# More buffers, a warm-up tile set by VectorE, a last tile ended in quarters, and new engine orders in a hybrid trunk layer

## The chip, the cores and the metric

The kernel runs on one core of one Trainium2 chip. The time is that of one execution on the device in microseconds (us), the median of several runs. Engines are called as in the profile: PE (TensorE), DVE (VectorE), ACT (ScalarE), POOL (GpSimd) and SP (SyncE, which issues the DMAs here).

## The reference

One layer over 1024 positions of width 1024, in float32. One projection gives the columns of three groups, each group's output is gated, and one output projection and a LayerNorm over the residual sum end the layer.

```python
proj = jnp.einsum("bsd,de->bse", x, w_in[l])
q, k, v, g_a, x_b, g_b, c_cols, g_c = jnp.split(proj, split_idx, axis=-1)
y_a = _swa_sinks(q, k, v, attn_sinks[l])      # 8 heads on 2 kv heads of 64, window 128, a sink per head
y_b = _rg_lru(x_b, ...)                       # causal convolution, gates, linear recurrence over time
y_c, v_own = _rwkv7(c_cols, ...)              # delta rule with a matrix state, 4 heads of 64
y = jnp.concatenate([y_a * silu(g_a), y_b * silu(g_b), y_c * silu(g_c)], axis=-1)
out = jnp.einsum("bse,ed->bsd", y, w_out[l])
x = _layer_norm(ALPHA * x + out, ln_g[l], ln_b[l])
```

## The kernel before

The 1024 positions are worked in two halves `h` of 512 columns, and the 1024 input rows in eight slices. Float32 products are made of rounded high parts and remainders: a product is three matmuls (high by high, high by low, low by high), so every activation (`xh`, `xl`) and every weight is split by a cast on ACT or DVE (`wcah`, `woh`) and a subtraction on DVE (`wcal`, `wol`).

*Start.* Four warm-up matmuls of 256 columns run on the tile `blocks`, which POOL sets; POOL makes of the same tile the block matrix `hsum`, used later for head sums. Behind them the seven tiles of the C group's projection (`c0`) are made straight from the loads, slice by slice. *Dense groups.* The remaining projections (tiles named `q0`, `ga0`, `xb1` and so on, in the order of the list `LISTED`) follow. In the first half their weights come into a raw tile (4 buffers), are split into a weight tile `w_...` (4 buffers) and written to DRAM; in the second half SP loads the split weights back from there (`w_ga<-kept_ga`, 512 KB each) as soon as a weight tile is free. *Side streams.* Among the dense matmuls lie the small ones. `scores_stream` makes scores of 128 queries (`sp`), masks them and sums them up in `mn` on DVE and takes the exponential on ACT into `s`; `turn_stream` transposes `s` on PE (`tp`) and puts the result, masked, into `PT`; `pv_stream` multiplies by the values (`pv`). The C group has per half eight chunks in series: a first `ch` from the state and the chunk's `X`, a copy to `u0`, a second `ch` with the transposed inverse `Tt`, a copy to `UV`, a third `ch` with `BKt`, and the new state `S`; `yp` is the chunk's output. The B group has its recurrence as a scan on DVE. The products with the output weights (`o`) and the normalisation of eight tiles of 128 positions (`finish`) end the program. The gates of a projection (`evac_gate`) and `PT` have fixed numbers of buffers, which set how far a stream may run ahead.

*Order.* Every helper records its instructions (`Listed`), so all rows carry line 231, or 253 in the changed kernel. The program is first written by `merge`, which draws from the streams by the string `MERGED`; then the table `ISSUED` gives, for every engine, the sequence of the recorded instructions, and each engine runs strictly by it. A matmul that must wait holds up all behind it on PE.

`finish` before:

```python
P.tensor_tensor(mv[:, 3:4], mv[:, 2:3], mhalf, op=ALU.pow)
for js in halves:
    V.scalar_tensor_tensor(xr[:, js], xr[:, js], mv[:, 0:1], lng[:, js], op0=ALU.subtract, op1=ALU.mult)
for js in halves:
    V.scalar_tensor_tensor(xr[:, js], xr[:, js], mv[:, 3:4], lnb[:, js], op0=ALU.mult, op1=ALU.add)
    SQ.dma_start(out[t0:t0 + 128, js], xr[:, js])
```

Of the kernel before, what the change touches and what calls it, by code (L numbers as in the profile page):

```python
# [10 lines left out]
F32 = mybir.dt.float32  # L11
# [10 lines left out]
T = 512  # L22
# [12 lines left out]
PVN = 2  # L35
C0 = (1, 4, 3, 0, 6, 2, 5)
# [10 lines left out]
NS = 3  # L47
NGATE = 2
# [1288 lines left out]
```

## Time and profile before

| | |
|---|---|
| median of 3 runs | 482.28 us (481.49 to 482.39) |
| profiled execution | 482.19 us |
| its span | 480.4 us |
| PE busy | 466.0 us, 97%, 3088 records |
| DVE busy | 364.7 us, 76% |
| ACT busy | 242.4 us, 50% |
| POOL busy | 36.4 us, 8% |
| bytes moved | 71.45 MB, 149 GB/s over the span |

Busy time is the sum of an engine's instructions in the span. Matmuls are pipelined: a record's duration is longer than the distance to the next one's start, so for PE the distances between starts are what counts. A line of the timeline may hold several equal instructions (x2, x8); its duration then covers them all. What stands in brackets is the idle time before and the instruction or transfer that ended it.

### The profile page before, as it was taken

The numbers are of one execution on the slowest core, as the hardware profiler recorded it, in microseconds if no ns is written. First come the engines' busy times: TensorE is split into PE (matmuls) and PEld (weight loads), VectorE is DVE, ScalarE is ACT, GpSimd is POOL, SyncE is SP. The second block draws the span as 40 slices with busy tenths as digits, with TensorE's granted clock in tenths as the row PEclk, the third lists the DMA queues.
The fourth block names the chain that finished last, engine by engine and source line by source line (L and its number), as shares of the span: only waits on it lengthen the run. The fifth ranks groups of instructions, "written<-read, shape, count | busy, mean of one in ns | idle before, by whom it ended". The sixth has DMA issues, their size and how long they took to land.

```text
span 480.4 us, 8435 instructions
## 1 busy us (share of the span) xinstructions
PE 466.0 (97%) x3088; PEld 360.8 (75%) x3088; DVE 364.7 (76%) x880; ACT 242.4 (50%) x544; POOL 36.4 (8%) x57
## 2 busy tenths in 40 slices
PE   8999999999999999999999998999999999999993
PEld 6777777777777776678778786787678778888893
DVE  5946798999998689737979669994868548636886
ACT  3427589434566798537694255329666546021000
POOL 0100000000000000000000000000002500054101
PEclk9999999999999999999999999999999999999997
DMA  8950537657766524233343484459420080120652
GB/s 275 386 200 0 196 136 264 199 130 262 268 238 130 189 91 132 89 114 128 99 167 88 141 233 153 132 119 220 134 67 24 16 283 32 64 69 0 219 176 87
DMA packets 50585, 71.45 MB, mean 149 GB/s; under 512 B 26344, under 2 KB 27624, under 8 KB 50544
## 3 DMA queue, kind: packets, MB, share of 16 engines
q1 hardware_dynamic: 50544, 70.91, 46.3%
q8 instruction: 24, 0.39, 0.4%
q14 instruction: 17, 0.14, 0.1%
HBM read 48.34 MB, written 22.56 MB: 148 GB/s over the span
## 4 chain that ended last, share of the span: by engine, by line
PE 74%; DVE 9%; ACT 7%; DMA 6%; issue 2%; SPq 1%; POOLq 0%; DVEq 0%; ACTq 0%
PE o L231 19%; PE pj_q L231 8%; PE pj_ga L231 6%; PE c L231 6%; PE pj_xb L231 3%; PE pj_gb L231 3%; PE pj_gc L231 3%; PE sp L231 3%; PE pv L231 3%; PE pj_v L231 2%; PE pj_r L231 2%; PE ch L231 2%; PE pj_av L231 2%; PE tp L231 2%; PE pj_k L231 2%
## 5 line engine op out<-in xcount | busy, mean ns | idle before, releaser
L231 PE MATMUL pj_ga<-xh,w_ga 128*128 128x512 f32 x128 | 44.0, 404 | 0.9 <-DMA w_ga<-kept_ga 0.9
L231 PE MATMUL pj_q<-xh,w_q 128*128 128x512 f32 x128 | 44.1, 403 | 0.5 <-DMA w_q<-kept_q 0.2
L231 ACT ACTIVATE s<-sp,mn 128x129 f32<-128x129 f32 x64 | 23.0, 366 | 22.0 <-DVE mn L231 21.7
L231 PE MATMUL o<-woh,yl 128*128 128x512 f32 (+1 forms) x90 | 32.5, 370 | 0.0
L231 PE MATMUL o<-woh,yh 128*128 128x512 f32 (+1 forms) x90 | 32.5, 375 | 0.0
L231 PE MATMUL o<-wol,yh 128*128 128x512 f32 (+1 forms) x90 | 32.3, 368 | 0.0
L231 PE MATMUL o<-wo,yh 128*128 128x512 f32 (+1 forms) x108 | 32.0, 374 | 0.0
L231 PEld LDWEIGHTS pj_ga<-xh,w_ga 128*128 128x128 f32 x128 | 23.6, 188 | 7.6 <-DVE it L231 1.2
L231 POOL TENSOR_TENSOR yl<-y,yh 128x512 fp32r<-128x512 f32 x16 | 20.3, 1291 | 118.0 <-PE pj_gc L231 105.5
L231 PEld LDWEIGHTS pj_q<-xh,w_q 128*128 128x128 f32 x128 | 23.8, 188 | 7.0 <-DMA w_q<-kept_q 0.7
L231 DVE SCALAR_TENSOR_TENSOR xres<-xres,o 128x512 f32<-128x512 f32 (+1 forms) x18 | 11.1, 624 | 20.3 <-PE o L231 16.2
L231 PE MATMUL pj_ga<-xl,w_ga 128*128 128x512 f32 x64 | 25.9, 405 | 0.0
L231 PE MATMUL pj_q<-xl,w_q 128*128 128x512 f32 x64 | 25.7, 401 | 0.0
L231 ACT ACTIVATE s<-s,mn 128x128 f32<-128x128 f32 x64 | 22.3, 398 | 4.3 <-DVE mn L231 4.1
L231 DVE SCALAR_TENSOR_TENSOR xres<-xres,mv,ln 128x512 f32<-128x512 f32 x32 | 22.6, 741 | 1.0 <-POOL mv L231 0.9
L231 PE MATMUL pj_gc<-xh,w_gc 128*128 128x512 f32 x64 | 23.1, 414 | 0.2 <-DVE q L231 0.2
L231 ACT CAST yh<-y 128x512 fp32r<-128x512 f32 x16 | 9.7, 618 | 26.6 <-PE o L231 22.1
L231 PEld LDWEIGHTS o<-wo,yh 128*128 128x128 f32 x108 | 19.4, 188 | 4.2 <-DVE wo L231 0.3
L231 PE MATMUL pj_gb<-xh,w_gb 128*128 128x512 f32 x64 | 21.8, 404 | 0.0
L231 PE MATMUL pj_xb<-xh,w_xb 128*128 128x512 f32 x64 | 21.8, 399 | 0.0
L231 DVE TENSOR_TENSOR PT<-tp,con 128x512 f32<-128x512 f32 x28 | 19.1, 684 | 3.4 <-PE tp L231 3.2
L231 PE MATMUL o<-wo,yl 128*128 128x512 f32 (+1 forms) x54 | 19.8, 369 | 0.0
(310 smaller groups left out, 1247.1 us busy)
## 6 DMA issues: line engine op xcount, KB each, us to landing
xr<-in_xT SPq DMA_DIRECT2D x16, 256.0 KB, 4.5
kept_ga<-w_ga SPq DMA_DIRECT2D x8, 512.0 KB, 3.2
kept_q<-w_q SPq DMA_DIRECT2D x8, 512.0 KB, 3.5
wor<-in_w_o SPq DMA_DIRECT2D x16, 256.0 KB, 2.8
w_q<-kept_q SPq DMA_DIRECT2D x8, 512.0 KB, 3.9
w_ga<-kept_ga SPq DMA_DIRECT2D x8, 512.0 KB, 4.4
xres<-in_x SPq DMA_DIRECT2D x8, 512.0 KB, 3.6
out<-xres SPq DMA_DIRECT2D x16, 256.0 KB, 2.2
```

What stands on the lines that cost most here:

```text
L231: self.ins.append(getattr(self.engine, op)(*args, **kw).ins)
```

## The change

The rings get more buffers: `PT` 4 to 6 (`PTB`, with the value tile `vt` and the output streams' use of the ring), scores `s` 3 to 5 (`NS`) and `mn` 4 to 6, gates 2 to 3, raw weights 4 to 5. The warm-up matmuls use a tile of their own, `warm`, set by DVE, and `blocks` shrinks to the 128 columns of `hsum`. In `finish` the last tile's second pass and its stores go by quarters of 256 columns. All lists of `ISSUED` but none of `MERGED` or `LISTED` are new; each engine gets the same work apart from the edits above (two more passes and stores, one more memset).

```diff
+PTB = 6
-NS = 3
-NGATE = 2
+NS = 5
+NGATE = 3
 ISSUED = {
 "tensor": (
-    "0-3 7 10-11 8 4-6 19-20 22-23 13 24-25 21 26 39-43 9 14-15 33-35 27 44-45 53-54 28-29 47 12 30-32 50-51 48 "
...
 "sync": (
-    "0 2 11 1 3-6 10 28 7-9 13 12 14-16 29-31 17-22 33 32 23-26 44-45 34 46 48 27 47 50 52 51 53-54 49 35-36 "
...
+    "0 2 1 10 3-4 28 5-9 13 29-30 14-15 12 16-17 31 18-23 11 34 24 32 44 25 46 26 48 27 33 47 50 45 52 35 54 49 "
...
-        return s(pers, "raw", shape, 4, F32, name)
+        return s(pers, "raw", shape, 5, F32, name)
...
-    blocks = s(first, "blocks", [128, 256], 1)
+    warm = s(first, "warm", [128, 256], 1)
+    V.memset(warm, 0.0)
+    blocks = s(first, "blocks", [128, 128], 1)
     P.memset(blocks, 0.0)
     for o in (0, 64):
         P.memset(blocks[o:o + 64, o:o + 64], 1.0)
 
     for _ in range(WARM):
-        TE.matmul(start_ps[6][:, 0:256], blocks[:, 0:128], blocks, start=True, stop=True)
-    P.tensor_copy(hsum, blocks[:, 0:128])
+        TE.matmul(start_ps[6][:, 0:256], warm[:, 0:128], warm, start=True, stop=True)
+    P.tensor_copy(hsum, blocks)
...
-        g = wt("gate", bufs=2, name=f"G_{name}_{h}")
+        g = wt("gate", bufs=3, name=f"G_{name}_{h}")
...
-    NS = 3
...
-        VT[0] = wt("PT", (128, T), 4, name=f"vt_{h}")
+        VT[0] = wt("PT", (128, T), PTB, name=f"vt_{h}")
...
-                    mn = wt("mn", (128, 4), 4, name=f"mn_{h}_{g}_{n}")
+                    mn = wt("mn", (128, 4), NS + 1, name=f"mn_{h}_{g}_{n}")
...
-            yield lambda: len(AQ) > i and len(BQ) - got("pv") + got("vt") < 4
+            yield lambda: len(AQ) > i and len(BQ) - got("pv") + got("vt") < PTB
...
-            PT = wt("PT", (128, 2, 2, 128), 4, name=f"PT_{h}_{g}_{n}")
+            PT = wt("PT", (128, 2, 2, 128), PTB, name=f"PT_{h}_{g}_{n}")
...
-        bufs = {"xs": XSB, "lt": 4, "q": 2, "PT": 4, "AR": 2, "rt": 6}
+        bufs = {"xs": XSB, "lt": 4, "q": 2, "PT": PTB, "AR": 2, "rt": 6}
...
-        for js in halves:
+        for js in quarters if (h, i) == (1, 3) else halves:
             V.scalar_tensor_tensor(xr[:, js], xr[:, js], mv[:, 3:4], lnb[:, js], op0=ALU.mult, op1=ALU.add)
             SQ.dma_start(out[t0:t0 + 128, js], xr[:, js])
```

Three places of the orders follow. Names end in a running number; `h` is the first number of a name behind its tag.

PE at the start of the program, before (`c0_1` to `c0_6` are tiles of the C projection, `wcah` the split weights of slice 0):

```order
L231 MATMUL c0_6_69<-blocks_76 128x256 x4
L231 MATMUL c0_2_70<-xh_0_0_95,wcah_0_89 128x512
L231 MATMUL c0_3_67<-xh_0_0_95,wcah_0_89 128x512
L231 MATMUL c0_3_67<-xl_0_0_96,wcah_0_89 128x512
L231 MATMUL c0_2_70<-xl_0_0_96,wcah_0_89 128x512
L231 MATMUL c0_1_65<-xh_0_0_95,wcah_0_89 128x512
L231 MATMUL c0_1_65<-xl_0_0_96,wcah_0_89 128x512
```

PE at the start, in the changed kernel:

```order
L253 MATMUL c0_6_69<-warm_76 128x256
L253 MATMUL c0_1_65<-xh_0_0_97,wcah_0_91 128x512
L253 MATMUL c0_6_69<-warm_76 128x256
L253 MATMUL c0_4_66<-xh_0_0_97,wcah_0_91 128x512
L253 MATMUL c0_6_69<-warm_76 128x256
L253 MATMUL c0_2_70<-xh_0_0_97,wcah_0_91 128x512
L253 MATMUL c0_3_67<-xh_0_0_97,wcah_0_91 128x512
L253 MATMUL c0_4_66<-xl_0_0_98,wcah_0_91 128x512
L253 MATMUL c0_2_70<-xl_0_0_98,wcah_0_91 128x512
L253 MATMUL c0_6_69<-warm_76 128x256
L253 MATMUL c0_6_69<-xh_0_0_97,wcbh_0_93 128x512
```

The four warm-up matmuls now read `warm` and stand one by one among the first matmuls of the C projection, instead of all ahead of them.

DVE at the start, in the changed kernel (`xh_0_0` and `xl_0_0` are the split of the first loaded slice):

```order
L253 MEMSET dv_410 128x1
L253 MEMSET carry_452 128x8
L253 MEMSET ec_425 128x2
L253 CAST xh_0_0_97<-xr_0_0_95 128x512
L253 MEMSET warm_76 128x256
L253 TENSOR_TENSOR xl_0_0_98<-xr_0_0_95,xh_0_0_97 128x512
```

The memset of `warm` is the fifth instruction of DVE, behind the first cast.

DVE around the copy of the transposed inverse `Tt` of the second half, before (`ti` and `tr` belong to the B group's recurrence, and the row `tr_1_1` with `hlast` is its scan):

```order
L231 SCALAR_TENSOR_TENSOR q3_1_3965<-pj_q3_1_3912,q3_1_3965 64x512 x2
L231 COPY u0_1_0_3716<-ch_1_0_3710 128x128
L231 SCALAR_TENSOR_TENSOR ti_1_1_3501<-ti_1_1_3501,xc_1_1_3470 128x512
L231 SCALAR_TENSOR_TENSOR tr_1_1_3500<-a_1_1_3506,hlast_452,ti_1_1_3501 128x512
L231 COPY Tt_1_3622<-tp_1_3634 32x16x32
L231 SCALAR_TENSOR_TENSOR y_1_5_3515<-tr_1_1_3500,G_gb1_1_3426 128x512
L231 SCALAR_TENSOR_TENSOR y_1_0_3577<-pv_1_0_3323,G_ga0_1_3558 128x512
```

DVE around the same copy in the changed kernel:

```order
L253 COPY_PREDICATED sp_1_2_0_3827<-con_63,sp_1_2_0_3827 128x2x128
L253 COPY sp_1_2_0_3827<-par_64 128x2
L253 TENSOR_REDUCE mn_1_2_0_3826<-sp_1_2_0_3827 128x2
L253 RECIPROCAL mn_1_2_0_3826<-mn_1_2_0_3826 128x2
L253 COPY u0_1_0_3718<-ch_1_0_3712 128x128
L253 SCALAR_TENSOR_TENSOR y_1_1_3757<-pv_1_1_3581,G_ga1_1_3744 128x512
L253 COPY Tt_1_3624<-tp_1_3636 32x16x32
L253 COPY_PREDICATED sp_1_2_1_3842<-con_63,sp_1_2_1_3842 128x2x128
L253 TENSOR_TENSOR PT_1_2_0_3873<-tp_1_2_0_3870,con_63 128x512
```

The scan, directly ahead of the copy before, stands 16 rows ahead of it now; between them are attention's masks and sums and the copy of `u0`.

PE at chunk 5 of the second half, from the chunk's first `ch` to its second, before:

```order
L231 MATMUL ch_1_5_4311<-UV_1_2989,X_1_2865 64x64 x4
L231 MATMUL yp_1_5_4312<-AR_1_0_2596,S_1_4_4283 64x64 x2
L231 MATMUL yp_1_5_4312<-AR_1_1_2853,S_1_4_4283 64x64 x2
L231 MATMUL tp_1_3_1_4047<-con_63,s_1_3_1_3987 128x128 x2
L231 MATMUL o_0_3_0_4492<-woh_4_0_3012,yh_0_4_4494 128x512
L231 MATMUL o_0_3_0_4492<-wol_4_0_3013,yh_0_4_4494 128x512
L231 MATMUL o_0_3_0_4492<-woh_4_0_3012,yl_0_4_4495 128x512
L231 MATMUL pv_1_3_4190<-PT_1_3_0_4020,vtok_457 64x128 x4
L231 MATMUL pv_1_3_4190<-PT_1_3_1_4050,vtok_457 64x128 x4
L231 MATMUL ch_1_5_4311<-u0_1_5_4317,Tt_1_3622 64x64 x4
```

PE at the same chunk in the changed kernel:

```order
L253 MATMUL ch_1_5_4313<-UV_1_2991,X_1_2867 64x64 x4
L253 MATMUL pj_gc0_1_4233<-xl_1_2_2328,w_gc0_1_0_4137 128x512
L253 MATMUL ch_1_5_4313<-u0_1_5_4319,Tt_1_3624 64x64 x4
L253 MATMUL pj_gc1_1_4234<-xh_1_3_2352,w_gc1_1_0_4168 128x512
L253 MATMUL o_0_1_0_4490<-woh_4_0_3014,yh_0_4_4496 128x512
L253 MATMUL pj_gc1_1_4234<-xl_1_3_2353,w_gc1_1_0_4168 128x512
L253 MATMUL o_0_1_0_4490<-wol_4_0_3015,yh_0_4_4496 128x512
L253 MATMUL o_0_1_0_4490<-woh_4_0_3014,yl_0_4_4497 128x512
L253 MATMUL pj_gc1_1_4234<-xh_1_3_2352,w_gc1_1_0_4168 128x512
L253 MATMUL yp_1_5_4314<-AR_1_0_2598,S_1_4_4285 64x64 x2
L253 MATMUL yp_1_5_4314<-AR_1_1_2855,S_1_4_4285 64x64 x2
L253 MATMUL ch_1_5_4313<-UV_1_2991,BKt_1_0_2965 64x64 x2
```

Between the two lay two `yp` pairs, two transposes, three `o` and eight `pv` matmuls; now there is one `pj_gc0` matmul, and the `yp` pairs stand behind.

## Rows read from the trace of the kernel before

**Rows 1.** The busy line of the profile page.

```profile
span 480.4 us, 8435 instructions
...
PE 466.0 (97%) x3088; PEld 360.8 (75%) x3088; DVE 364.7 (76%) x880; ACT 242.4 (50%) x544; POOL 36.4 (8%) x57
```

**Rows 2.** PE's timeline, 0 to 8 us: start, duration, operation, count, [idle before <-releaser].

```profile
1.48 3.78 PE L231 MATMUL c<-blocks 128*128 128x256 f32 x8 [1.48 <-POOL blocks L231]
5.00 1.22 PE L231 MATMUL c<-xh,wcah 128*128 128x512 f32 x2
...
7.30 0.44 PE L231 MATMUL c<-xl,wcah 128*128 128x512 f32 x1
7.58 0.39 PE L231 MATMUL c<-xh,wcal 128*128 128x512 f32 x1
7.81 0.40 PE L231 MATMUL c<-xh,wcbh 128*128 128x512 f32 x1
```

**Rows 3.** PE's timeline, first late start of the middle.

```profile
86.73 0.39 PE L231 MATMUL pj_q<-xh,w_q 128*128 128x512 f32 x1
87.38 1.16 PE L231 MATMUL sc<-AR,BK 64*128 64x128 f32 x16 [0.26 <-DVE AR L231]
```

**Rows 4.** PE's timeline, 338 to 342 us.

```profile
338.89 0.63 PE L231 MATMUL pj_ga<-xh,w_ga 128*128 128x512 f32 x2
340.26 0.35 PE L231 MATMUL ch<-u,Tt 64*64 64x64 f32 x5 [0.74 <-issue]
...
340.83 0.50 PE L231 MATMUL pj_ga<-xl,w_ga 128*128 128x512 f32 x1
341.17 0.62 PE L231 MATMUL pj_ga<-xh,w_ga 128*128 128x512 f32 x2
341.63 0.39 PE L231 MATMUL pj_ga<-xl,w_ga 128*128 128x512 f32 x1
341.95 0.45 PE L231 MATMUL ch<-UV,BKt 128*64 128x64 f32 x8
```

**Rows 5.** DVE's timeline, the last normalisation.

```profile
474.61 0.15 DVE L231 TENSOR_SCALAR mv<-mv 128x1 f32<-128x1 f32 x1
...
475.85 1.41 DVE L231 SCALAR_TENSOR_TENSOR xres<-xres,mv,ln 128x512 f32<-128x512 f32 x2 [0.44 <-POOL mv L231]
```

**Rows 6.** DVE's timeline, the first cast.

```profile
3.46 0.43 DVE L231 CAST xh<-xr 128x512 fp32r<-128x512 f32 x1 [2.43 <-DMA xr<-in_xT]
```

**Rows 7.** ACT's timeline, the first weights' cast.

```profile
4.43 0.51 ACT L231 CAST wcah<-wca 128x384 fp32r<-128x384 f32 x1 [2.43 <-DMA wca<-in_w_c]
```

**Rows 8.** PE's timeline, 16 to 18 us.

```profile
16.33 0.40 PE L231 MATMUL c<-xh,wcbh 128*128 128x512 f32 x1
17.18 0.50 PE L231 MATMUL c<-xh,wcal 128*128 128x512 f32 x1 [0.45 <-DVE wcal L231]
```

**Rows 9.** DMA issues of the page: count, KB each, median us to landing.

```profile
w_q<-kept_q SPq DMA_DIRECT2D x8, 512.0 KB, 3.9
w_ga<-kept_ga SPq DMA_DIRECT2D x8, 512.0 KB, 4.4
...
out<-xres SPq DMA_DIRECT2D x16, 256.0 KB, 2.2
```

**Rows 10.** PE's timeline, 296 to 298 us.

```profile
296.26 0.47 PE L231 MATMUL pj_xb<-xh,w_xb 128*128 128x512 f32 x1
297.63 0.47 PE L231 MATMUL pj_ga<-xh,w_ga 128*128 128x512 f32 x1 [0.90 <-DMA w_ga<-kept_ga]
```

**Rows 11.** DVE's timeline, 338 to 340 us.

```profile
338.15 1.28 DVE L231 TENSOR_TENSOR_SCAN tr<-a,hlast,ti 128x512 f32<-128x512 f32 x1
339.47 0.69 DVE L231 COPY Tt<-tp 32x512 f32<-32x512 f32 x1
```

**Rows 12.** PE's timeline, a chunk's first matmuls.

```profile
167.88 0.45 PE L231 MATMUL ch<-UV,X 128*64 128x64 f32 x8
```

**Rows 13.** ACT's timeline, the copy that answers.

```profile
168.38 0.27 ACT L231 COPY u<-ch 128x128 f32<-128x128 f32 x1
```

More of the change, by code (lines that the diff above doesn't have):

```diff
@@ L68 @@
 "tensor": (
[55 rows of a table removed]
[74 rows of a table added]
 ),
 "vector": (
[29 rows of a table removed]
[30 rows of a table added]
 ),
 "scalar": (
[16 rows of a table removed]
[16 rows of a table added]
 ),
 "gpsimd": (
-    "0 2 1 3-4 14-15 5-13 17 16 27-28 18-24 26 25 29-37 41-48 39 38 40 49-52"
+    "0 4 1-3 5-8 15 9-12 14 16-17 13 18-19 27-28 20-24 26 25 29-36 41-44 37 45-46 38 47-48 39-40 49-52"
 ),
 "sync": (
[6 rows of a table removed]
[7 rows of a table added]
 ),
```

230 rows, old and new, of the table ISSUED are left out of this document.

## The prediction

> **What bounds the kernel now.** I read the busy line first: PE is busy 97% of a span of 480.4 us, DVE 76% [rows 1]. The profiled execution took 482.19 us, that is 1.8 us around the span, and the median of the runs shown is 482.28, so its sum can stand for the median. With PE that full, the time is the number and rate of its matmuls plus the time in which it stands. Their number does not change (2460 instructions in both programs), so I went through PE's own timeline for four things: the start, where matmuls run at half rate; the end, where PE has finished; the places in the middle where the next matmul starts later than the one before allows; and the price of changing between wide and small matmuls.
>
> *Start.* PE waits 1.48 us for the POOL memset of `blocks`; then the warm-up runs, eight passes of about 0.43 us each [rows 2]. The first 512-column matmul starts at 5.00 and the sixth at 7.30, so 0.46 apart; from 7.58 on they are 0.23 apart. These are the lower and the higher of the clock's two levels (1.2 and 2.4 GHz); before the rise PE had been at work since 1.48 without a stop. *Middle.* At full level a 512-column matmul follows another after 0.234 us. Between 86 and 340 us there are 20 places where the next starts over 0.2 us later than that; together they are 8.2 us. First and last are [rows 3, 4]: 87.38 after 86.73, and 340.26 after a matmul at about 339.12 (0.90 late). From 400 to 470 us there are none. *End.* The last normalisation runs on DVE and POOL and its stores take the span 3.1 us beyond DVE's end (477.26 [rows 5]).
>
> **The change part by part.** Start from 482.19.
>
> *Warm-up from a VectorE tile.* The memset of `warm` is on DVE, but in the new order it stands behind the cast of `xh_0_0`, which waits for a load and ran 3.46 to 3.89 [rows 6]. So the first warm-up can start at about 4.1 instead of 1.48, and its four matmuls (0.86 us each at half rate) stand between the first real ones, which need ACT's cast of `wcah` (4.43 to 4.94 in the order before [rows 7]) anyway. If the clock still rises at about 7.4, 3.3 us are left at half rate: two warm-ups, two real matmuls and most of the third warm-up, where before five real ones were done by 7.30. Late by 3 to 3.3 matmuls of 0.234 (0.8), the rest of the third (0.1) and the fourth at full rate (0.4): **+1.3**. If the rise moves as far as the first matmul does (2.6 us, so to 10.0), six real matmuls are done by then against fifteen: nine times 0.234, +2.2. Against this, PE's wait at 16.33, where the next matmul starts 0.85 later because DVE's `wcal` is late [rows 8], may go, since a later PE lets DVE catch up: between 0 and -0.6. Ends +0.7 and +2.2; I take +1.3, the row's time of rise unchanged. The load of `con`, third on SP's queue before, moves behind the first weights; its first reader on PE is a transpose some 200 rows into the order, so it costs nothing.
>
> On what the rise hangs, the row can't tell: PE was at work from 1.48, and the rise came at 7.3. The Trainium skill, "TensorE: Matmul & The Clock Gate", Part 1, holds that the throttled level is the default and that activity releases it; this speaks against a warm-up that starts 2.6 us later. The trace agrees in so far as the early matmuls run at half rate. By that rule the rise would come later and the term would be the +2.2; by the row alone it is the +1.3.
>
> *Tail.* `mv`'s epsilon row was at 474.61, behind a half of the first pass; DVE then waited for POOL's power and did the second pass from 475.85 on, 1.41 us for two halves [rows 5]. In the new order the epsilon comes directly behind the aggregation, one half of the first pass (0.7) earlier, so the power is done by about 475.2. One half of the first pass and the four quarters, 0.7 and four times 0.35 to 0.4, are then still to do: DVE ends at 477.3 to 477.5 where it ended at 477.3, but the last store carries 128 KB instead of 256, and a 256 KB store lands 2.2 us after its issue [rows 9]. **-0.3**, between 0 (a store's time is mostly fixed) and -0.6.
>
> *The new order: switches.* A small matmul starts 0.32 behind a wide one (341.63 to 341.95) instead of 0.234, and the next wide one behind the first wide one after a small block 0.34 (340.83 to 341.17) [rows 4]: 0.19 for a block of small ones. Blocks of small matmuls between wide ones (single transposes left out) are 77 in the order before and 84 in the new: 7 x 0.19 = **+1.3**, between 0 and +2 as a count from an order can be off.
>
> *The new order: waits that go.* Of the 8.2 us the largest are two. At 296.26 the next matmul starts 1.37 later; PE waits 0.90 for `w_ga`, which the queue can load only when a slot of weights is free [rows 10]. There are 13 wide matmuls between the slot's last use and its next first use; in the new order 35, that is 9.4 us instead of 4.8 for a load that takes 4.4 [rows 9]; `w_ga0_1_1` gets 11.9 for 3.9, and `w_q1_1_1` 22.5 for 4.0. The wait goes whole. At 340.26 PE waited for DVE's copy of `Tt`, started at 339.47 behind the scan of 338.15 (1.28 us) [rows 4, 11]. In the new order the scan stands 16 rows ahead of the copy. This goes too. The other 18 (0.2 to 0.6 each) are handovers from ACT or DVE to PE in the attention and the delta-rule chain; the second is what more buffers of scores and transposed scores are for: `tp` to `pv` is mostly looser in the new order. I let three quarters of all go: **-6.2**. Ends: nothing (rival 2) and -8.2.
>
> *The new order: waits that come.* Where chunk's first `ch` goes to the copy `u` and back to `ch`, the copy is done 0.8 us after the first `ch` started (167.88 to 168.38 + 0.27 [rows 12, 13]). At 5 of the 16 chunks the new order puts only 0.2 to 0.4 us of other matmuls between (least before: 0.6); each costs 0.2 to 0.5, so 1.0 to 2.5. The scores (`sp`) come nearer to their transposes (`tp`): median 8 to 6.3 us of PE work, four under 4 where the path through DVE and ACT takes 3.4 to 3.9: up to 0.4 each. Behind a waiting `ch` everything else on PE waits. **+2.5**, between 1 and 4.
>
> *Buffers alone* (raw weights 5, gates 3) add no instruction; a raw slot or a gate earlier free can only start a load or an ACT row earlier, at no cost where DMA is far from full. Their worth is in the order that they permit, counted above.
>
> Sum: 482.19 + 1.3 - 0.3 + 1.3 - 6.2 + 2.5 = **480.8**.
>
> **The rivals.** *1, on the other side: kept weights arrive late.* In the second half the seven next-tightest weights of the new order have 3.8 to 4.5 us between a freed slot and first use (`gc0`, `ak`, `gb1` twice, `gb0`, `q3`, `xb0`); landing takes 3.9 to 4.4 [rows 9]. The order before had six with 3.9 to 4.4 and only some of them waited, which speaks against. For it: work comes 7 to 15 us earlier, so loads of `w_o` and the residual fall in the same stretch and a landing can be longer. It decides as soon as landing with queueing passes 4.3 us: 0.4 to 1.1 for each of seven, 3 to 5 in all: 483.2 to 486. *2: the change does not do what it says.* The waits are latencies of handovers that an order only shifts elsewhere: what goes in one place comes in another, so that -6.2 and +2.5 cancel: 482.19 + 1.3 - 0.3 + 1.3 = 484.5 (484 to 486.5 with a late rise). For it: 97% busy leaves little, and 18 of the 20 waits are below 0.6. *3: cold head.* The clock rises at 10 and not at 7.4, and the 16.33 wait remains or is replaced: 480.8 + 0.9 and up to 0.6 more = 481.7 to 482.3, which is no change. For it: the work that PE did ahead of the rise now begins 2.6 us later. *4: more goes.* All 8.2 go, and the tight chain places cost under 1: 482.19 + 2.3 - 8.2 + 0.5 to 1 = 476.8 to 477.3, with the 16.33 wait gone also 476.2.
>
> **How the numbers follow.** A measurement of this kernel can tell about 0.2% (1 us) from no change: faster is below 481.3, slower above 483.2. The forecast (478.5 to 481.3) has 0.33, rival 4 (476 to 478.5) 0.11, so faster 0.44. No change has 0.21: 0.11 from rival 3, 0.10 from the forecast's own terms at their worse ends. Slower has 0.35: rival 1 0.20, rival 2 0.15. The range that leaves about 2 in 10 out goes from 476.5 (the early end of rival 4) to 486.0 (the upper end of rival 1); the forecast's own range is 478.5 to 481.3.
>
> **What would show it.** In the profile of the changed kernel: the first warm-up at about 4.1, the first 0.23 spacing at 7.4 (or near 10.0: rival 3); the `w_ga` wait and the one before `ch<-u,Tt` gone, so PE idle behind DMA below 0.3 in the second half; new idle of 0.2 to 0.5 before `ch<-u,Tt` at five chunks; PE's last output matmul about 1.1 us earlier than before; the epsilon directly behind the last aggregation and a last store of 128 KB. Wrong it is if PE waits behind kept weights over 1 us in sum after 250 us (rival 1), if the sum of late starts in the middle is still 8 us with no DMA in it (rival 2), or if the end of PE is earlier but the tail longer.

## The result and the profile after

The changed kernel took 490.21 us (median of 4 runs, 488.56 to 490.46) beside 482.33 for the kernel before on the same chip: 1.0154 times as long, 95% interval 1.0129 to 1.018. The forecast was 480.8, faster, with a range up to 486.0. It is slower, by more than the worst rival allowed for.

Profile page of the changed kernel: its span and the busy line. Behind them PE's last matmul, in the changed kernel and in the kernel before.

```profile
span 488.5 us, 8454 instructions
...
PE 466.7 (96%) x3088; PEld 362.0 (74%) x3088; DVE 366.1 (75%) x883; ACT 239.5 (49%) x544; POOL 36.8 (8%) x57
```

```profile
480.25 0.28 PE L253 MATMUL o<-woh,yl 128*128 128x256 f32 x1
```

```profile
472.41 0.28 PE L231 MATMUL o<-woh,yl 128*128 128x256 f32 x1
```

The profiled execution took 490.31. PE does the same work as in [rows 1] in 8.1 us more. The last matmul starts at 480.25 where it started at 472.41, so 7.8 of the 8.1 are lost ahead of PE's end and 0.3 behind it.

PE's timeline of the changed kernel at the start (start, duration, operation, count, what ended the idle time before):

```profile
4.21 1.22 PE L253 MATMUL c<-warm 128*128 128x256 f32 x2 [4.21 <-DVE warm L253]
4.87 0.99 PE L253 MATMUL c<-xh,wcah 128*128 128x512 f32 x1
...
7.43 1.41 PE L253 MATMUL c<-xh,wcah 128*128 128x512 f32 x2
8.64 1.05 PE L253 MATMUL c<-xl,wcah 128*128 128x512 f32 x2
...
9.99 0.62 PE L253 MATMUL c<-xh,wcbh 128*128 128x512 f32 x1
...
10.68 0.39 PE L253 MATMUL c<-xl,wcah 128*128 128x512 f32 x1
```

This answers to [rows 2]. The first warm-up is at 4.21, forecast 4.1. The wide matmuls (512 columns) at 8.64 are still 0.43 apart, from 10.68 on they are 0.23 apart. By 20 us 48 wide matmuls have started, before it were 55: 7 times 0.234 = 1.6. A part of this belongs to the one execution: two kernels further down start in the same way, the one with a square in place of a root and the one with the light inverse, and there 52 and 50 wide matmuls have started by 20 us.

PE in the second half, where the longest new wait is:

```profile
300.82 0.40 PE L253 MATMUL pj_ga<-xl,w_ga 128*128 128x512 f32 x1
303.28 0.39 PE L253 MATMUL sp<-KH,q 128*128 128x256 f32 x1 [2.06 <-ACT s L253]
...
304.91 0.63 PE L253 MATMUL pj_ga<-xl,w_ga 128*128 128x512 f32 x1
305.33 0.63 PE L253 MATMUL pj_ga<-xh,w_ga 128*128 128x512 f32 x1
...
307.04 0.40 PE L253 MATMUL pj_ga<-xl,w_ga 128*128 128x512 f32 x1
```

Engine sums of that stretch (window, length, PE busy, granted clock, DMA share, GB/s):

```profile
303.28:307.20 3.92, 3.92 (x12) 0.56 0.44 118
```

The scores at 303.28 waited 2.06 us for ACT's exponentials, and behind the wait the granted clock is 0.56: wide matmuls stand 0.43 apart until 307.04. So this one place cost twice: 2.2 of standing and some seven wide matmuls by 0.2, 1.4. What ACT and VectorE did there:

```profile
298.88 1.28 ACT L253 ACT_TABLE_LOAD   x1
300.17 0.63 ACT L253 ACTIVATE xc<-xc 128x512 f32<-128x512 f32 x1
301.13 1.28 ACT L253 ACT_TABLE_LOAD   x1 [0.32 <-DVE mn L253]
302.42 0.37 ACT L253 ACTIVATE s<-sp,mn 128x129 f32<-128x129 f32 x1
```

```profile
299.18 0.69 DVE L253 SCALAR_TENSOR_TENSOR q<-pj_q,q 64x512 fp32r<-64x512 f32 x1
299.90 0.43 DVE L253 COPY_PREDICATED sp<-con,sp 128x256 f32<-128x256 uint32 x1
...
300.63 0.42 DVE L253 TENSOR_REDUCE mn<-sp 128x2 f32<-128x258 f32 x1
```

ACT makes the square root of the B group (300.17) between exponentials and loads its function table twice for that, 1.28 us each. The maximum `mn` that the exponential needs comes from VectorE at 301.05, behind the split of a query, 299.18, and steps of the inverse (`it`, `TW`). The second load starts at 301.13, when this maximum is there; the first and the square root are over by 300.80. So only one of the two loads lies between the maximum and the exponential.

PE's waits in the whole span, summed by what ended them (us in total, times, longest):

```profile
PE sp L253 <- ACT s L253: 3.0, 3, 2.1
PE bt L253 <- ACT BKt L253: 1.3, 2, 0.7
PE vp L253 <- DVE BKt L253: 0.9, 1, 0.9
PE pj_ga L253 <- DVE G_gb L253: 0.7, 1, 0.7
...
PE pj_gc L253 <- DMA w_gc<-kept_gc: 0.3, 1, 0.3
```

The transfers are no longer among the first: 0.3 us. The waits are for ACT and VectorE.

The end, to be held against [rows 5]:

```profile
481.78 0.15 DVE L253 TENSOR_SCALAR mv<-mv 128x1 f32<-128x1 f32 x1
481.85 0.74 DVE L253 SCALAR_TENSOR_TENSOR xres<-xres,mv,ln 128x512 f32<-128x512 f32 x1
483.03 2.46 DVE L253 SCALAR_TENSOR_TENSOR xres<-xres,mv,ln 128x256 f32<-128x256 f32 x5 [0.43 <-POOL mv L253]
```

The epsilon row does follow at once (481.78), but only one half of the first pass is left to do until the power comes, VectorE waits 0.43, and five rows follow: a quarter, the other half of the first pass, and three quarters.

Where the middle's time went, counted over every pair of neighbouring matmuls from 25 us on in both traces: the places over 0.2 us late (22 in this count, 8.8 us, in the kernel before) shrank to 1.6 us at the same instructions. In the changed kernel 32 places are late, 15.8 us in all (the slow stretch's 0.2 each not among them), at instructions which in the kernel before were late by 2.3 in sum. So 7.2 went, and 13.5 came. With the start's 1.6 and the slow stretch's 1.4 that makes 9.3; the 7.8 at PE's end are less by 1.5. The changes of size gave back some 0.4 of that (see the part on switches below); where the rest came back is not known.

### The profile page after: what moved, and what is told of

It is laid out like the page before. It is cut to its first block, busy times and chain, and to the rows that moved or that the text cites. A ratio compares the mean times of both kernels' runs of the same rounds, so it can differ in the third digit from the quotient of the medians.

```text
span 488.5 us, 8454 instructions
## 1 busy us (share of the span) xinstructions
PE 466.7 (96%) x3088; PEld 362.0 (74%) x3088; DVE 366.1 (75%) x883; ACT 239.5 (49%) x544; POOL 36.8 (8%) x57
## 4 chain that ended last, share of the span: by engine, by line
PE 69%; DVE 17%; ACT 9%; issue 2%; DMA 2%; POOLq 0%; DVEq 0%; ACTq 0%
PE o L253 18%; PE c L253 9%; PE pj_ga L253 6%; PE pj_q L253 4%; PE pj_gc L253 3%; PE ch L253 2%; PE pj_v L253 2%; PE pj_r L253 2%; PE pj_k L253 2%; PE pj_av L253 2%; PE pj_gb L253 2%; PE sp L253 2%; PE pj_xb L253 2%; PE pv L253 2%; PE yp L253 2%
## 5 line engine op out<-in xcount | busy, mean ns | idle before, releaser
L253 PE MATMUL pj_ga<-xh,w_ga 128*128 128x512 f32 x128 | 47.5, 416 | 1.3 <-DVE G_gb L253 0.7
L253 PE MATMUL o<-wo,yh 128*128 128x512 f32 (+1 forms) x108 | 34.8, 369 | 0.0
L253 PE MATMUL o<-woh,yl 128*128 128x512 f32 (+1 forms) x90 | 31.2, 370 | 0.0
L253 PE MATMUL o<-woh,yh 128*128 128x512 f32 (+1 forms) x90 | 30.9, 370 | 0.0
L253 ACT ACTIVATE s<-s,mn 128x128 f32<-128x128 f32 x64 | 23.5, 401 | 3.9 <-DVE mn L253 3.8
L253 DVE SCALAR_TENSOR_TENSOR xres<-xres,mv,ln 128x512 f32<-128x512 f32 (+1 forms) x34 | 23.1, 712 | 1.5 <-POOL mv L253 1.3
L253 PE MATMUL pj_xb<-xh,w_xb 128*128 128x512 f32 x64 | 23.0, 402 | 0.2 <-DVE G_gb L253 0.2
L253 PE MATMUL sp<-KH,q 128*128 128x256 f32 (+1 forms) x64 | 17.8, 299 | 3.6 <-ACT s L253 3.0
```

The lines of the kernel that those rows point to most:

```text
L253: self.ins.append(getattr(self.engine, op)(*args, **kw).ins)
```

## The experiments

Ratios are to the kernel before, run beside each on the same chip, with 95% intervals. "Old order" means the kernel before's sequences of all engines. Both programs have the same 2460 matmuls in their lists, so a matmul of one trace has its counterpart in another; "the same matmul" is meant so below. `bt` and `vp` are transpositions of the C group on PE, `bo` is one of its head sums.

**Is it the rings, the other edits, or the order?** The ring sizes alone:

```diff
-NS = 3
+NS = 5
-        return s(pers, "raw", shape, 4, F32, name)
+        return s(pers, "raw", shape, 5, F32, name)
...
```

> The kernel before with the new ring sizes alone (PT 6, scores 5, mn 6, gates 3, raw weights 5), its own order of the engines unchanged. Theory one (the new order of instructions is what costs): every engine still runs the old sequence, a free buffer earlier changes nothing that PE waits for, so 482.3, within 1 us. Rival (larger rings let transfers and ACT rows start earlier and collide): 484 or more. Rival (the rings gain by themselves and the order loses more than the sum shows): 480 or less.

481.49 us, 0.9985 (0.9976 to 0.9994). And all edits with the old order (warm tile's memset first on VectorE, quarters, both halves of the first pass ahead of them):

> The changed kernel with all its edits (rings, warm tile set by VectorE, last tile in quarters) but with the old sequences of the engines; the memset of the warm tile stands first on VectorE, and at the end the epsilon directly behind the aggregation, then both halves, then the four quarters. Theory one (the new order costs): 482.3 less up to 0.6 at the end and up to 0.5 at the start, so 481.2 to 482.3. Rival (one of the edits itself costs, the quarters or the warm tile): 484 or more.

481.19 us, 0.9981 (0.9973 to 0.999). The rings and the small edits together are worth about 0.9 us. So the whole loss, 9 us against this kernel, comes from the new sequences.

**The start.** In the changed kernel's order:

```diff
 "tensor": (
-    "0 4 1 13 2 7 10 14 8 3 19-20
+    "0-4 13 7 10 14 8 19-20
...
 "vector": (
-    "55 80 56 1 0 2 45
+    "0 55 80 56 1-2 45
```

> The changed kernel, the memset of the warm tile moved to VectorE's first place and the four warm-up matmuls to PE's first places, all else as in the changed kernel. By 20 us the changed kernel had started 7 matmuls of 512 columns fewer than the kernel before, 7 times 0.234 = 1.6. Theory (what is lost at the start is never made up, since PE is nearly always busy): 490.2 less 1.6 to 2.1, 488.1 to 488.6. Rival (PE would only wait longer later, for work that VectorE and ACT hand over): 489.7 to 490.2.

489.15 us, 1.0144 (1.0128 to 1.0159): 1.1 less, between the two expectations; this interval and the changed kernel's overlap, so the 1.1 by itself is not clear of noise. In its trace 59 wide matmuls have started by 20 us, 11 more, which is 2.6 us. The same matmul starts 2.4 us earlier than in the changed kernel's trace at 20 us, 3.1 at 150, 1.9 at 170 and 0.8 from 360 us on. So about as much as was gained at the start is lost later, at three places. The first, 1.1, is a stretch at the lower clock that the changed kernel's trace does not have, with no wait above 0.25 ahead of it (two views: PE's timeline, then window, length, PE busy, granted clock, DMA share, GB/s):

```profile
156.17 1.37 PE L257 MATMUL tp<-Tt,Gp 32*32 32x32 f32 x64
...
158.58 0.34 PE L257 MATMUL ch<-UV,X 128*64 128x64 f32 x4 [0.25 <-ACT X L257]
```

```profile
159.30:162.60 3.30, 3.30 (x17) 0.50 0.72 243
```

The other two are waits at 330 (0.6) and 354 us (0.5). PE's waits have for the first of them a row that the changed kernel had not:

```profile
PE pj_ga L257 <- DMA w_ga<-kept_ga: 0.9, 1, 0.9
```

The old order with a late warm-up tells what a late start is worth by itself:

```diff
 "vector": (
-    "0 56-57 79 81 78 55 80 1-2
+    "56-57 79 81 78 55 80 1 0 2
```

> All edits with the old order, but the memset of the warm tile behind VectorE's first cast, where the changed kernel has it; PE's four warm-up matmuls, still first in its order, then start at 4.2 in place of 1.2. Theory (the late start costs in itself, and the clock rises as much later): the rise near 10, some 9 matmuls of 0.234 fewer by then, of which the wait of 1.1 at 8.2 hides a part: 481.2 plus 1.0 to 2.1 = 482.2 to 483.3. Rival (the rise stays where it was, and the loads limit the first 17 us anyway): 481.2 to 481.6.

483.44 us, 1.0026 (1.0001 to 1.005), with single runs from 480.69 to 487.22. The sum is just above the theory's range, but not for its reason. PE's timeline, with the same stretch of the old order with an early warm-up behind it:

```profile
4.12 3.78 PE L236 MATMUL c<-warm 128*128 128x256 f32 x8 [4.12 <-DVE warm L236]
7.34 1.06 PE L236 MATMUL c<-xh,wcah 128*128 128x512 f32 x2
...
8.71 0.40 PE L236 MATMUL c<-xh,wcah 128*128 128x512 f32 x1
```

```profile
8.15 0.40 PE L236 MATMUL c<-xh,wcah 128*128 128x512 f32 x1
9.62 0.50 PE L236 MATMUL c<-xh,wcah 128*128 128x512 f32 x1 [1.07 <-ACT wcah L236]
```

The clock is up by 8.71, not near 10. The early start ran into a wait of 1.07 at 9.62 for weights that were still being loaded; the late one did not. By 20 us both have started 53 wide matmuls: here the late warm-up cost nothing. Of the 3.7 us that the profiled execution (484.53) lost, 2.7 go at 301.26, where the scores stood 1.91 us and ran at the lower clock until 304.7:

```profile
301.26 0.47 PE L236 MATMUL sp<-KH,q 128*128 128x256 f32 x1 [1.91 <-ACT s L236]
...
302.17 1.05 PE L236 MATMUL pj_ga<-xh,w_ga 128*128 128x512 f32 x2
```

So in these traces the start matters where loads come early enough to use it, as in the new order, which loads the constants later.

**The place at 299.** One function changed, without a table load:

```diff
-        A.activation(a2, a2, AF.Sqrt)
+        A.activation(a2, a2, AF.Square if (h, p) == (1, 0) else AF.Sqrt)
```

> The changed kernel with one ACT row replaced: the square root of the B group's first tile in the second half is a square, which needs no table load (this part of the output is left wrong, the row's length stays). The two table loads of 1.28 us at 298.88 and 301.13 go. In the changed kernel PE stood 2.06 us behind ACT's exponential there and ran the next 3.4 us at the lower clock, about eight matmuls by 0.2 more each. Theory (two loads cause the wait, and the wait the lower clock): 490.2 less 2.2 and 1.6 = 486.4. Rival A (loads cause the wait, but the clock falls for another reason): 487.9. Rival B (VectorE's maxima for the scores are late anyway, the loads only stand in their shadow): 489.5 to 490.2.

487.15 us, 1.0111 (1.0097 to 1.0125): 3.1 less, between the theory and rival A.

```profile
299.38 0.39 PE L257 MATMUL pj_ga<-xl,w_ga 128*128 128x512 f32 x1
300.57 0.39 PE L257 MATMUL sp<-KH,q 128*128 128x256 f32 x1 [0.80 <-ACT s L257]
...
301.03 0.39 PE L257 MATMUL pj_ga<-xh,w_ga 128*128 128x512 f32 x1
```

The wait falls from 2.06 to 0.80 and the stretch at the lower clock is gone: 1.3 and 1.4 are 2.7. The 1.3 are one load and not the theory's two, as only the second stood behind the maximum. The remaining 0.8 is rival B's: VectorE's maximum is late by itself. That the medians differ by 3.1 has some chance in it: the same matmul is already 1.4 earlier than in the changed kernel's trace ahead of the place (299.38 and 300.82), 0.8 of it since the first 10 us, where the clock rose earlier in this execution, which the edit cannot have caused. It is 3.9 earlier behind the place, which is 2.5 for the place, and 3.2 at the end. The Trainium skill, "ScalarE: Activation LUTs", section "What ACT_TABLE_LOAD costs", adds a drain of about the same length to each load; no such second piece shows here: the square root starts 1.29 us behind the start of its load, the exponential 1.29 behind its own.

**Does a wait by itself bring the lower clock?** Copies on ACT between two exponentials in the old order, at the scores for which PE waits anyway:

```diff
+    for _ in range(3):
+        A.copy(scratch, con[:, 0:512])
```

> All edits with the old order, and one copy of 128x512 on ACT (about 0.6 us, result unused) between the two exponentials for which PE's next scores wait 0.8 us at 298.3. Theory (a wait of PE costs its length, and only a long one the clock): a wait of 1.4, no stretch at the lower clock, 481.2 plus 0.6 = 481.8. Rival (there is slack on PE's side): 481.2. With a fall of the clock: 483.4.

> The same with three copies, 1.7 us in all: a wait of 2.5 us, as long as the changed kernel's at 300.82. Theory (such a wait brings the lower clock behind it, also in the old order): 481.2 plus 1.7 plus 1.6 = 484.5, with PE's wide matmuls 0.43 apart for some 3 us behind the wait. Rival (the fall in the changed kernel came from something else): 482.9, all wide matmuls 0.23 apart.

One copy: 481.72 us, 0.9994 (0.9976 to 1.0012), most runs at 481.0 to 481.9 and two at 484.3 and 484.6; the profiled one is of these two, and its trace has a wait of 2.17 and a stretch of 3 us at the lower clock behind it. Three copies: 484.0 us, 1.0038 (1.0022 to 1.0055). PE's timeline and the granted clock of the stretch with three:

```profile
297.33 0.39 PE L236 MATMUL pj_ga<-xl,w_ga 128*128 128x512 f32 x1
301.41 0.58 PE L236 MATMUL sp<-KH,q 128*128 128x256 f32 x1 [3.70 <-ACT s L236]
...
302.43 1.05 PE L236 MATMUL pj_ga<-xh,w_ga 128*128 128x512 f32 x2
```

```profile
301.60:307.00 5.40, 5.40 (x15) 0.50 0.27 74
```

The lower level (0.50) holds for 5.4 us behind a wait of 3.70. So such a fall does not need the new order. It does not come each time either. In the sixteen profiled executions of all kernels here, the granted clock as a mean over the span is 0.989 to 0.993 in the seven that have such a stretch in the middle, and 0.994 to 0.998 in the nine that have none. By this mark the fall came in two of the eight runs with one copy, in six of the ten with three, and in three of the four of the changed kernel (the fourth is the one of 488.56). With the late warm-up it came in four of ten, which took 484.5 to 487.2 us; the other six took 480.7 to 484.0. The same scores' wait was 1.91 in the profiled run with the late warm-up and 0.80 in the one with the early warm-up; why it is longer there is open. And the run with the warm-up first, above, shows a fall with no long wait ahead of it. So a wait is one way to it, and not the only one. The Trainium skill, "TensorE: Matmul & The Clock Gate", section "HAM oscillation — how this bites in real kernels", tells of waits for transfers after which matmuls run slow again; the rows here show this behind waits for ACT.

**Can the new order's waits be taken one by one?** Groups of small matmuls later on PE, on top of the two edits above; the diff shows the two `bt`, and `vp_0_0` with `vp_0_1`, `sp_1_0_0` (its second pair), `sp_1_0_3`, `sp_1_2_2`, `sp_1_3_2`, the first four of `ch_0_0` and `bo_0_1` are moved in the same way:

```diff
 "tensor": (
...
-    1278-1280 1284 1281 1379-1380 1282 1285 1283 1381-1383 1286 1384-1387 1287 1388-1389
+    1278-1279 1379-1382 1280-1283 1383-1386 1284-1287 1387-1389
```

> The changed kernel with the warm-up first (as in the run before), the square in place of the one square root in the second half (output left wrong there), and eight groups of small matmuls that waited put 2 to 8 wide matmuls later in PE's order: vp of the first half (1.2 of wait), two bt of the second half (1.6), three groups of scores of tile 0 and 2 (0.6, 1.0, 0.6), scores of tile 3 (0.7, two wide ones later), the first ch of the first half (0.8), bo (0.5). The other engines' orders stay. The two edits measured alone gave 1.1 and 3.1, so without the eight 486.0. Theory (the new order's loss is the sum of places where a small matmul stands too close behind its producer on VectorE or ACT): six of the 6.6 go, 480 to 481. Rival (VectorE and ACT are late by themselves in this order, the wait turns up at the next handover): 484.5 to 486.

487.03 us, 1.0103 (1.008 to 1.0126): the theory falls, there is no gain in sum. The trace tells gains and losses apart, beside that of the run with the square alone. At the two `bt` 1.2 is gained. The 0.9 of `vp` has become a wait of 1.56 at 100.46. And at 158.97, where the four `ch` were put later, the transposition that stood behind them now comes first and waits 1.32 for ACT, with the lower clock behind it: 1.6 is lost there. So the sum of nothing is a gain and a loss.

**Is VectorE too full?** Sums of 20 us (window, length, then busy time and count of PE, weight loads, VectorE, ACT and POOL, clock, DMA share, GB/s), before and after:

```profile
60.00:80.00 20.00, 20.00 (x108) 15.24 (x108) 18.75 (x37) 17.52 (x30) 1.02 (x4) 1.00 0.58 200
...
280.00:300.00 20.00, 18.83 (x100) 15.09 (x98) 16.46 (x50) 9.26 (x31) 0.00 (x0) 1.00 0.61 193
300.00:320.00 20.00, 19.87 (x113) 15.69 (x114) 18.80 (x65) 5.57 (x18) 0.00 (x0) 1.00 0.44 132
```

```profile
60.00:80.00 20.00, 19.31 (x96) 14.14 (x94) 19.86 (x38) 11.18 (x19) 2.30 (x7) 1.00 0.60 220
...
280.00:300.00 20.00, 19.26 (x91) 14.75 (x90) 18.67 (x56) 10.75 (x20) 0.00 (x0) 1.00 0.43 146
300.00:320.00 20.00, 17.94 (x95) 13.87 (x94) 17.32 (x55) 12.56 (x43) 0.00 (x0) 0.91 0.36 104
```

VectorE is busy 18.67 of 20 us at 280 to 300 where it was 16.46: the B group's recurrence of the second half now falls into the same stretch as the inverse and the scores. At 60 to 80 it was nearly full before, and is a little more so now; at 300 to 320 it is the other way round. So VectorE is not fuller on the whole, and whether its fullness costs anything has to be tried. The inverse cut short, in both orders:

```diff
-            n, m = 31 - sI, sI // 2 + 1
+            n, m = 31 - sI, 1
```

> The changed kernel, in which the 62 small VectorE rows per half that invert the triangular matrices work on one column in place of up to 16 (the inverse, and so the C group's output, is left wrong); all instructions and orders stay. In the changed kernel VectorE is busy 93 to 99% from 60 to 140 and from 280 to 300 us, and PE's longest waits stand there. Theory (a full VectorE is what hands over late in the new order, so that waits only move when PE's order is mended): shorter rows there take away the late handovers of scores at 290 to 303 with the lower clock behind, and some at 95 to 135: 490.2 less 4 = 486, at least 2 more than the old order gains by the same edit. Rival (each handover's own latency decides, not how full VectorE is): 489 to 490.2.

> The same edit of the inverse (output left wrong in the same way) in the kernel with all edits and the old order. Theory (VectorE full): the old order has VectorE at 82% from 280 to 300 and one wait of 1.0 there: 481.2 less 1 to 1.5 = 479.7 to 480.2. Rival (handover latency): 481.2.

New order 485.14, 1.0058 (1.0042 to 1.0073); old order 480.62, 0.9965 (0.9954 to 0.9976). The new order gains 5.1, more than the theory's 4; the old one 0.6, between its two expectations. The place at 299 is among the 5.1: its scores are 0.4 late there and no slow stretch follows, so about 3.2 of the 5.1 (1.8 of the wait, 1.4 of the clock) are that place. Of the rest 0.4 is an earlier rise of the clock at the start, and the others are handovers behind VectorE. This leaves open whether the spread groups would now help. Two runs asked it, on the light inverse with the warm-up first:

> The changed kernel with the short rows of the inverse (485.1 alone; the C group's output is left wrong) and the warm-up first (worth 1.1 alone). If the start's gain is kept where VectorE has room: 485.1 less 1.1 to 2.4 = 482.7 to 484.0. If it is waited away later: 484.5 to 485.

> The same and the eight groups of small matmuls put 2 to 8 wide matmuls later in PE's order, as in the run where they did not help. Theory (a full VectorE kept those waits alive): now the waits of bt, ch, vp, bo and of the scores go for good, 3 to 4.5 less than the run with the same edits without the spreading: 479 to 480.5. Rival (what is put later delays its own successors, whatever room VectorE has): within 1 us of the run without the spreading.

483.78, 1.0038 (1.0025 to 1.0051), and 484.51, 1.0051 (1.0034 to 1.0068). The start's gain is kept now (1.4), but the spreading again gains nothing in sum. By place it is as before: 1.5 is gained at the two `bt`, and 1.6 lost at 158.36, where the transposition waits and the clock falls, in the trace of the last run:

```profile
158.36 0.33 PE L256 MATMUL tp<-con,s 128*128 128x128 f32 x1 [1.32 <-ACT s L256]
```

```profile
159.00:162.30 3.30, 3.30 (x24) 0.50 0.74 235
```

The mean granted clock is 0.991 to 0.993 in all five runs with the spreading and 0.994 to 0.997 in all six without it, so the fall came each time here. The rival holds in sum, but not for each wait: those of `bt` can be taken singly, that of `ch` was exchanged for a longer one with the lower clock behind it, and that of `vp` is a link of a chain. `vp` put later makes VectorE's rows on it later, the convolution behind them later, the PSUM bank of `pj_xb` free later, and the next gate projection waits, in the same trace:

```profile
98.76 0.40 PE L256 MATMUL pj_ga<-xh,w_ga 128*128 128x512 f32 x1
100.72 0.50 PE L256 MATMUL pj_ga<-xh,w_ga 128*128 128x512 f32 x1 [1.57 <-DVE past L256]
```

**A kernel that beats both.** The old order has single waits as well. Two attempts, each on the kernel with all edits and the old order, first:

```diff
 "vector": (
...
-    723 689 663-664 685 665
+    723 689 685 663-665
...
 "sync": (
-    "0 2 11 1 3
+    "0 2 1 3
...
-    22 33 32 23
+    22 33 11 32 23
```

In the first attempt both lists are changed (663, 664 and 685 are the two rows of the recurrence and the copy, 11 the constants).

> All edits with the old order, and two instructions moved: VectorE's copy of the transposed inverse of the second half ahead of the scan that stood before it (PE waited 0.9 there), and the load of the constants from SP's third place to its 28th, as in the new order (PE waited 1.1 for ACT's cast of the third slice's weights). Without these two 481.2. Theory (the old order has a few single waits left that can be taken one by one): 479.3 to 480.3. Rival (what is waited for is late anyway: the load because of the transfer rate of the first 10 us, the copy because of its PE producer): 481 to 481.5.

480.48 us, 0.9965 (0.9951 to 0.9979). The load of the constants, costed at nothing in the prediction, gave 59 wide matmuls by 20 us in place of 53, 1.3 us; in the profiled execution 1.0 of this is lost again at 330.16, in a wait for a transfer. The copy gave nothing: its wait of 0.9 went, and one of 0.8 and one of 0.4 came within the next 8 us of PE. In the second attempt the copy stands where it stood, and mask, sink and maximum of one block of scores (614 to 616) go ahead of two steps of the inverse, and one subtraction (14) ahead of another:

```diff
 "vector": (
-    62-63 42 64 14 16
+    62-63 14 42 64 16
...
-    560-561 569-571 614-615 572 616 577
+    560-561 614-616 569-572 577
```

> All edits with the old order; the load of the constants in SP's 28th place as in the run before, the copy of the transposed inverse back in its old place, and two moves on VectorE: mask, sink and maximum of the scores of tile 0, block 3 of the second half ahead of two steps of the inverse that stood before them (PE waits 1.0 to 1.4 for them), and the subtraction for the third slice's weights ahead of that of a table not needed yet (PE waits 0.6). Theory: 480.5 less 0.6 and less about 1 = 479.0 to 479.6. Rival (as with the copy in the run before, what goes at one place comes at the next): 480.5 to 481.

480.15 us, 0.9965 (0.9952 to 0.9977): 1.8 us below the kernel before, less of a gain than the theory had. The ratio is that of the first attempt, so the two moves on VectorE cannot be told from nothing. The scores' wait is gone; one of 0.92 stands 7 us later at a transposition, and the 1.2 gained at the first is lost at the second.

## Why the prediction was wrong

**The step that failed** is "the new order: waits that come", +2.5 with bounds 1 and 4. It measured 13.5. I had counted new tight places in two chains only, the handovers of `ch` to `u` and of scores to transposes, and took everything else as loose because PE's distances looked loose. The waits came elsewhere: scores behind ACT (3.0 in the list of waits), `bt` (1.3), `vp` (0.9), gates (0.7). Of the `ch` to `u` handovers that I priced at 0.2 to 0.5 at five chunks, one of 16 is over 0.2 late. What I did not do was to lay VectorE's and ACT's own rows beside PE's: the order shows that the recurrence and its square root fall into the scores' stretch, and the rows of before show what a scan and a split take. The sum also had no term for a clock that falls in the middle; in the profiled execution that was another 1.4.

**Waits that go**, -6.2: right. Those of the kernel before fell by 7.2, the two large ones, `w_ga` and `ch<-u,Tt`, among them [rows 4, 10]. A term can be right and the sum wrong, if what comes is priced from a shorter list than what goes.

**The start**, +1.3 with an upper end of 2.2: the clock was up near 10, as the rival had it, and 1.6 were lost by 20 us. That the rise stays at 7.4 when the first matmul comes later holds in no trace; it moves with the first matmul, as the +2.2 had it, but with a scatter that neither of my two rules allows for. With the first matmul at 1.48 the wide ones are 0.23 apart from 7.58 on in the kernel before and from 6.31 on with the new rings; with the first at 4.21 to 4.24, from 10.45, 10.07 and 8.24 on in three kernels with the same start. So the 1.6, and its being near +1.3, are in part luck: the other two of these have 50 and 52 wide matmuls by 20 us, 0.7 to 1.2 us less than before. The chance of a cold head was there; its result "no change" was not, since the middle decided.

**The end**, -0.3: it measured +0.3. The power is earlier, but a half of the first pass that filled the wait before now stands behind a quarter that waits for the power, which my reading of the new order had missed. With the old order and all edits, where both halves stand ahead of the quarters, the span ends 7.7 us behind PE's last matmul in place of 8.0, which is the -0.3.

**Switches**, +1.3: not seen, and both factors were wrong. The count was 77 to 84 blocks; the traces have 156 changes from a wide to a small matmul in place of 112 (from 20 us on). At 0.19 each that would be far more than 1.3, but what they add up to, where no place is over 0.2 late, is 5.4 in place of 5.8. So that the term did little harm is luck.

**Rivals.** Kept weights late (3 to 5): wrong in the changed kernel, 0.3 in all; only where the start was mended do one or two of them stand at 0.7 to 1.1. "What goes in one place comes in another" was nearest in kind and I held it to a cancelling sum, 484.5; it can be more than that, as a wait can bring the lower clock behind it, which no rival had.

**What stays open.** Old order and new differ by 9.0 us. The place at 299 with its lower clock (2.5 by the trace, 3.1 by the medians), the further room on VectorE (about 1.9: the 5.1 less that place, measured together only), the start (1.1 to 1.4, not clear of noise) and the two `bt` (1.2 to 1.5, by two traces) explain some 7 to 8. What is left is put down to waits of chains such as `vp` and `ch`, which is argued and not shown: moving PE's rows alone did nothing there or brought the lower clock, and an order with VectorE's and ACT's rows moved along with them was not tried. It is open too why the clock falls at a place in one execution and not in the next.

## What to carry to other kernels

When every engine's order is replaced, price the waits that come from the orders of the producers, row against row on VectorE and ACT, and not from how far apart two rows stand on the full engine. Wider rings by themselves moved 0.6 us: they permit an order, and the order has to be tested alone. A wait on a full PE is not the unit of account: with the lower clock behind it, 2.2 us of standing became 3.6 here. And when a trial of several moves gives nothing in sum, compare the two traces place by place: here a gain of 1.5 and a loss of 1.6 looked like nothing.

## What the runs showed of the hardware

That a wait in the middle of a PE-bound kernel brings the lower clock was not expected: granted 0.56 for 3.9 us behind a wait of 2.06, 0.50 for 5.4 us behind one of 3.70, 0.50 for 3.3 us behind one of 1.32. It does not come each time: with one copy on ACT in two of eight runs, by their times and their mean granted clock. Once it came with no wait above 0.25 ahead of it (159.30 to 162.60, the run with the warm-up first), behind 64 matmuls of 32x32 and two short waits; three other kernels with the same rows and about the same waits there kept the full clock. The rise at the start moves with the first matmul but scatters: wide matmuls 0.23 apart from 8.24, 10.07 and 10.45 on in three kernels whose start is the same.
